# Down projection by seven products for 20 of its 43 k tiles, with earlier state loads, moved cache copies and two output tiles in two parts

## The chip, the cores and the metric

The kernel runs on one core of one Trainium2 chip. The metric is the device time of one execution in microseconds (us); less is better. The times before are 2527.97, 2526.18 and 2524.59 us, median 2526.18.

## What is computed

One inference step of one decoder layer in fp32, for a prompt of 512 tokens and 8 samples of 4 tokens (544 rows in all). Cut to what matters here:

```python
y = concat([o_a, o_b]) @ w_out            # o_a: gated linear attention, o_b: dilated attention
h = h + y                                 # D_MODEL = 2048
up = rmsnorm(h) @ w_up                    # 2048 -> 2 * 5504
full = concat([conv_hist, up])            # state: the last two rows
conv = conv_b + sum(conv_w[j] * full[:, j:j + t] for j in range(3))
u, g = split(conv)
h = h + (silu(g) * u) @ w_down            # 5504 -> 2048
y = rmsnorm(h)
k_s, v_s = old cache rows shifted by 4, with the new rows behind them   # new caches of the samples
```

Outputs are y, the attention states and caches, and the convolution's state.

## The kernel before

Activations lie transposed, 128 features on the partitions and 544 rows (NT) along the free axis, in two halves of 272 columns (HT). Each fp32 matrix product is made of three products of rounded parts: weights and activations are split into a high part (ACT, whi or ah, L190) and a low part (DVE, wlo or al, L191), and PE adds hi x hi, hi x lo and lo x hi. One k tile (128 rows of a weight) against one output tile (128 columns) so costs 3 x 2 matmuls of 128x272. PE loads weights (PEld) beside the matmuls.

The program runs through input projection and attention (to about 880 us), the output projection over 16 output tiles (gemm, L219, matmuls in L225, to about 1061), the transition to the FFN, the FFN's 43 up-projection tiles (class Pair, to about 1985) and the down projection over 16 output tiles (to about 2514), with the final norm at its end.

The output projection loads xT into h (L935), adds the product (L936), stores h to the scratch tensor hscr (L937) and starts one copy of old cache rows with every second tile (keep_rows, L631; a copy is a DMA of 3060 KB from DRAM to DRAM on POOL's queue; sixteen in all, six of them here).

The FFN works by seven products instead of eight (Pair, L977): two blocks of the weight are summed before the product, by an SP load of one block and an accumulating load of the other on POOL's queue (load, L983 to L991), or by DVE (rs + ra, rs + raw). The operand of product T3, called M below, is the block sum W(0,0) + W(1,0), loaded into raw and accumulated there. Before the first tile, the constants vcv (L1086) and the states ci (L1101) are loaded; F takes ci in (L1028), and V (L1038) is the copy of a finished product that frees its PSUM bank for the next. Each finished tile a is stored to a scratch tensor adr (L1121), 43 in all; a store and the loads that follow are ordered by semaphores.

The down projection first takes three k tiles that were kept in SBUF (KEPT, 288 matmuls, L1152 to L1156), and meanwhile loads others from adr into ar on SP's queue (fetch, L1138 to L1141) and splits them into dh and dl. Then three groups of 16, 16 and 8 k tiles follow, each over all 16 output tiles: weights come through raw (three buffers) and raw3 (two), and in the first group the stored h comes back as hr (L1201 to L1203, SP's queue).

The order of the instructions on each engine comes from a scheduler with priorities (high_priority in the code); each engine executes its own list in order, and a DMA queue belongs to the engine that issues it (SP: q1, POOL: q0).

Of the kernel before, what the change touches and what calls it, by code (L numbers as in the profile page):

```python
# [17 lines left out]
P = 128  # L18
# [24 lines left out]
GATES_FIRST = 4  # L43
POOL_SPLIT = 6
NKEPT = 3
NSLOT = 11
FW = 2 + TP + NB * (2 + TS)


# [74 lines left out]
def _build(tc, nc, es, xT, st_gla, ck, cv, conv_in, vecs, w_in, w_gu, w_out, w_up, w_dn,  # L124
           t_cs, t_bp, t_masks, t_scan, t_small,
           yT, gla_p, gla_s, kT_p, k_s, vT_p, v_s, conv_out):
    def opened(*args, **kw):
        p = tc.tile_pool(*args, **kw)
        return p, p.__enter__()
# [17 lines left out]
    def hv(t):  # L147
        return t.rearrange("p (a b) -> p a b", a=2)
# [148 lines left out]
    def gps():  # L297
        return pg.tile([P, 2, 512], F32, tag="g", name="g")
# [596 lines left out]
    def factors(some, X, pool):  # L895
# [24 lines left out]
        for i in some:  # L920
# [3 lines left out]
            else:  # L924
                parts(i, T3, 2, b[i][:, 1:3])

    X = {}
    for ot in range(KD):
        ps = gps()
        gemm(ps, [wpart(w_out, order[:8], ot * P), wpart(w_out, order[8:], ot * P)], og)  # L930
        i, j = divmod(ot, 2)
        if j == 0:
            hp = HX.tile([P, 2, NT], F32, tag="h", name="h", bufs=KD // 2 + 1 - AHEAD)
        ht = hp[:, j]
        nc.gpsimd.dma_start(ht, xT[ot * P:(ot + 1) * P, :])  # L935
        nc.vector.tensor_add(hv(ht), hv(ht), ps[:, :, :HT])  # L936
        nc.gpsimd.dma_start(hscr[ot], ht)  # L937
        if ot == 0:
            nc.scalar.activation(acc2, ht, AF.Square)
        else:  # L940
            sq = htmp("sq")
            nc.scalar.activation(sq, ht, AF.Square)
            nc.vector.tensor_add(acc2, acc2, sq)
        X[i] = hp
        if ot % 2 == 1 and kept_rows:
            keep_rows()
        nc.scalar.activation(ht, ht, AF.Copy, scale=vec[:, V_FFN + ot:V_FFN + ot + 1])
        if j == 1 and i < AHEAD:
            factors([i], X, VA)
# [132 lines left out]
    nc.scalar.activation(rstdF[:, 2:2 + TP], rstd[:, :TP], AF.Copy)  # L1082
    nc.scalar.activation(rstdF[:, 2 + TP:].rearrange("p (b s) -> p b s", s=2 + TS)[:, :, 2:],
                         rstd[:, TP:].rearrange("p (b t) -> p b t", t=TS), AF.Copy)
    vcv = FP.tile([P, NVEC - V_CW], F32, name="vcv")
    nc.gpsimd.dma_start(vcv, vecs[:, V_CW:])  # L1086

    ci_v = conv_in.rearrange("p (s f) r -> p s f r", s=2)
    co_v = conv_out.rearrange("p (s f) r -> p s f r", s=2)
    def sv(x):  # L1090
        return x[:, 2 + TP:].rearrange("p (b s) -> p b s", s=2 + TS)[:, :, :TS]

    KEPT = list(range(KF - 1 - NKEPT, KF - 1))
    kept = {}
    ci = co = None
    for f, pr in enumerate(pairs):
        if f % 4 == 0:
            n = min(4, KF - f)
            ci = FP.tile([P, 2, 4, 2 * NB], F32, tag="ci", name="ci", bufs=2)
            co = FP.tile([P, 2, 4, 2 + 2 * NB], F32, tag="co", name="co", bufs=2)  # L1100
            nc.gpsimd.dma_start(ci[:, :, :n, :], ci_v[:, :, f:f + n, :])  # L1101
# [29 lines left out]
    taken = [0]

    def slot(n=0):

        pool = DS2 if n else DS
        return pool.tile([P, NT], F32R, tag="dh", name="dh"), pool.tile([P, NT], F32R, tag="dl", name="dl")

    def fetch(k, n):  # L1138
        hi, lo = slot(n)
        x = DS.tile([P, NT], F32, tag="ar", name="ar", bufs=2)  # L1140
        nc.sync.dma_start(x, adr[k])  # L1141
        split(hi, lo, x)
        return hi, lo

    h = [None] * KD
    A1 = {}
    rest = [k for k in range(KF) if k not in KEPT]
    groups = [rest[:16], rest[16:32], rest[32:]]
    with tc.high_priority(offset=min(1500, tc.cur_priority - P0)):
        for k in groups[0][:NSLOT]:  # L1150
            A1[k] = fetch(k, 0)
    for ot in range(KD):  # L1152
        ps = gps()
        gemm(ps, [wpart(w_dn, KEPT, ot * P)], kept)
        h[ot] = rows.tile([P, NT], F32, tag="R", name="h")
        nc.scalar.activation(hv(h[ot]), ps[:, :, :HT], AF.Copy)  # L1156
    closed(g0_p, re_p, va_p)
    ds2_p, DS2 = opened(name="ds2", bufs=24 - NSLOT, side="right")
    w3_p, W3 = opened(name="w3", bufs=1, side="right")
    even = [0]  # L1160

    def wraw():
        even[0] ^= 1
        if even[0]:
            return wts.tile([P, 8, P], F32, tag="raw", name="raw", bufs=3)
        return W3.tile([P, 8, P], F32, tag="raw3", name="raw3", bufs=2)

    def ctile(name):
        return W3.tile([P, NT], F32, tag="c", name=name, bufs=2)

    def wheld(w, ks, c0, n):

        raw = wraw()
        wload(raw, w, ks, c0)
        out = []
        for j in range(2):
            hi, lo = [t[:, :4 * P].rearrange("p (k c) -> p k c", k=4) for t in slot(n[j])]
            r = raw[:, 4 * j:min(4 * j + 4, len(ks)), :]
            m = r.shape[1]
            split(hi[:, :m], lo[:, :m], r)  # L1180
            out.append([(ks[4 * j + x], hi[:, x, :], lo[:, x, :]) for x in range(m)])
        return out


    where = {}
    pool_of = [0] * NSLOT + [1] * (24 - NSLOT)
    for i, k in enumerate(rest):
        where[k] = pool_of[i % 24]
    used = len(rest)
    for gi, ks in enumerate(groups):  # L1190
        A = {}
        with tc.high_priority(offset=min(2000, tc.cur_priority - P0)):
            for k in ks:
                A[k] = A1[k] if k in A1 else fetch(k, where[k])
        if gi < len(groups) - 1:
            for ot in range(KD):
                ps = gps()
                gemm(ps, [wpart(w_dn, ks[i:i + 8], ot * P) for i in range(0, len(ks), 8)], A)
                nc.vector.tensor_add(hv(h[ot]), hv(h[ot]), ps[:, :, :HT])
                if gi == 0:  # L1200
                    x = W3.tile([P, NT], F32, tag="hr", name="hr", bufs=1)  # L1201
                    nc.sync.dma_start(x, hscr[ot])
                    nc.vector.tensor_add(h[ot], h[ot], x)  # L1203


    tc.keep_in_program_order(nc.scalar.preload_act_table_set("natural_log_exp_and_others"))
# [32 lines left out]
        finish(ot, ps, 0, 2)  # L1239
    held = []  # L1240
    for i in range(HK):
        held.append(wheld(w_dn, ks, (HK + i) * P, [pool_of[(used + 2 * i + j) % 24] for j in range(2)]))
    for s in range(2):
        for ot in range(HK, KD):
            ps = gps()
# [3 lines left out]
        for ot in range(KD):  # L1249
# [5 lines left out]
    closed(w3_p, ds2_p, ds_p, rows_p, wu_p, wts_p, psu_p, psg)  # L1255


# [64 lines left out]
```

## Time and profile before

| | |
|---|---|
| median of three runs | 2526.18 us |
| profiled execution | 2525.10 us |
| its span | 2523.3 us |
| mean granted clock of TensorE | 0.991 |
| PE busy | 2462.7 us, 19479 matmuls |
| DVE, ACT, POOL busy | 1619.3, 1078.8, 435.3 us |
| moved by DMA | 427.73 MB, mean 170 GB/s |

The span is the profiled execution from its first to its last instruction; 1.8 us of the execution's own time lie around it. A row of a table of stretches gives each engine's busy time in a window; PEclk is the granted clock as a share of 2.4 GHz, and the DMA share is the mean busy share of the core's 16 DMA engines. A wait is named by the engine that waited and by the instruction whose end released it. The landing time of a DMA runs from its issue to the arrival of its last byte.

### The profile page before, as it was taken

The page shows a single profiled execution, that of the slowest core. Times are in us where ns is not written, and L with a number is a line of the kernel's source. Part 1 is how long each engine was busy: PE and PEld are TensorE (multiplying, and loading weights), DVE is VectorE, ACT ScalarE, POOL GpSimd, SP SyncE. Part 2 cuts the span into 40 slices and gives each one's busy share as a digit, 9 for nine tenths or more (in the row PEclk, how much of TensorE's full clock was granted, in tenths as well). Part 3 has the DMA queues.
Part 4 walks back from the last instruction along what each step waited for, and adds up shares of the span by engine and source line. Part 5 has one row for each costly group of instructions (what it writes and reads, how often), then busy time and mean ns, then how long its engine had stood idle before and what let it go on. Part 6 is the DMA issues. An engine that isn't in the chain of part 4 may idle for free.

```text
span 2523.3 us, 47163 instructions
## 1 busy us (share of the span) xinstructions
PE 2462.7 (98%) x19479; PEld 2385.2 (95%) x19479; DVE 1619.3 (64%) x2460; ACT 1078.8 (43%) x1870; POOL 435.3 (17%) x581
## 2 busy tenths in 40 slices
PE   8999999999999899989999999999999999999997
PEld 8988887899999899989999999999999999999997
DVE  7777764267777843478878888888888643342243
ACT  6344464133334433355555555555555531131142
POOL 1333434210002320112212221222121000000001
PEclk9999999999999999999999999999999999999999
DMA  7777744544555498668888888889888473443232
GB/s 220 197 202 197 193 114 138 161 131 141 166 177 177 159 305 256 169 146 192 192 188 192 191 191 189 191 191 192 189 191 178 124 219 107 115 151 92 85 100 72
DMA packets 581593, 427.73 MB, mean 170 GB/s; under 512 B 18976, under 2 KB 553728, under 8 KB 580608
## 3 DMA queue, kind: packets, MB, share of 16 engines
q1 hardware_dynamic: 462144, 248.31, 34.9%
q0 software_dynamic: 115200, 171.02, 30.1%
q10 hardware_dynamic: 4032, 5.38, 0.6%
q8 instruction: 153, 2.51, 0.4%
q14 instruction: 64, 0.52, 0.1%
HBM read 397.40 MB, written 77.37 MB: 188 GB/s over the span
## 4 chain that ended last, share of the span: by engine, by line
PE 82%; DMA 8%; DVE 6%; issue 2%; POOL 1%; ACT 1%; SPq 0%; DVEq 0%; POOLq 0%; ACTq 0%
PE g L225 40%; PE b L965 20%; PE g L965 15%; DMA q<-qscr 6%; DVE pr L411 1%; PE v L507 1%; PE s L673 1%; DMA ar<-adr 1%; DVE wlo L191 1%; DVE kv L412 1%; PE s L561 1%; DMA xr<-in_xT_dram 0%; PE s L548 0%; PE s L795 0%; POOL q L408 0%
## 5 line engine op out<-in xcount | busy, mean ns | idle before, releaser
L191 DVE TENSOR_TENSOR wlo<-raw,whi 128x1024 fp32r<-128x1024 f32 (+1 forms) x341 | 408.3, 1198 | 295.6 <-ACT whi L190 288.7
L190 ACT ACTIVATE whi<-raw 128x1024 fp32r<-128x1024 f32 (+1 forms) x345 | 355.0, 1030 | 555.1 <-PE g L225 454.0
L225 PE MATMUL g<-ah,whi 128*128 128x272 f32 x2048 | 442.9, 296 | 9.8 <-ACT ah L190 4.6
L225 PE MATMUL g<-al,whi 128*128 128x272 f32 x2048 | 447.2, 297 | 0.5 <-DVE al L191 0.5
L225 PE MATMUL g<-ah,wlo 128*128 128x272 f32 x2048 | 442.4, 295 | 0.3 <-DVE wlo L191 0.3
L965 PE MATMUL b<-vh,whi 128*128 128x272 f32 x1376 | 395.1, 288 | 6.2 <-ACT V L1038 4.8
L965 PE MATMUL b<-vl,whi 128*128 128x272 f32 x1376 | 395.9, 289 | 0.8 <-DVE vl L893 0.6
L965 PE MATMUL b<-vh,wlo 128*128 128x272 f32 x1376 | 389.9, 288 | 1.3 <-DVE wlo L191 1.3
L225 PEld LDWEIGHTS g<-ah,whi 128*128 128x128 f32 x2048 | 327.9, 191 | 19.7 <-issue 10.3
L225 PEld LDWEIGHTS g<-al,whi 128*128 128x128 f32 x2048 | 329.2, 191 | 11.6 <-issue 9.3
L225 PEld LDWEIGHTS g<-ah,wlo 128*128 128x128 f32 x2048 | 328.3, 190 | 10.2 <-issue 8.5
L965 PE MATMUL g<-vl,whi 128*128 128x272 f32 x1032 | 298.8, 290 | 2.0 <-DVE vl L893 1.9
L965 PE MATMUL g<-vh,whi 128*128 128x272 f32 x1032 | 297.8, 289 | 0.4 <-ACT vh L892 0.3
L965 PE MATMUL g<-vh,wlo 128*128 128x272 f32 x1032 | 296.8, 288 | 0.0
L965 PEld LDWEIGHTS b<-vh,whi 128*128 128x128 f32 x1376 | 260.0, 189 | 6.7 <-ACT V L1038 5.1
L225 PE MATMUL g<-dh,whi 128*128 128x272 f32 x1248 | 258.0, 288 | 4.1 <-ACT whi L190 2.7
L965 PEld LDWEIGHTS b<-vl,whi 128*128 128x128 f32 x1376 | 259.5, 189 | 1.5 <-DVE vl L893 1.5
L965 PEld LDWEIGHTS b<-vh,wlo 128*128 128x128 f32 x1376 | 257.4, 189 | 1.5 <-DVE wlo L191 1.5
L225 PE MATMUL g<-dh,wlo 128*128 128x272 f32 x1248 | 258.2, 288 | 0.0
L225 PE MATMUL g<-dl,whi 128*128 128x272 f32 x1248 | 258.1, 288 | 0.0
L190 ACT ACTIVATE whi<-rs 128x1024 fp32r<-128x1024 f32 x129 | 136.8, 1061 | 266.8 <-PE g L965 201.1
L225 PEld LDWEIGHTS g<-dh,whi 128*128 128x128 f32 x1248 | 195.7, 188 | 5.4 <-ACT whi L190 3.4
(341 smaller groups left out, 4101.5 us busy)
## 6 DMA issues: line engine op xcount, KB each, us to landing
raw<-in_w_up_dram SPq DMA_DIRECT2D x129, 512.0 KB, 4.1
raw<-in_w_in_dram SPq DMA_DIRECT2D x96, 512.0 KB, 4.8
raw<-in_w_dn_dram SPq DMA_DIRECT2D x64, 512.0 KB, 4.0
out_k_s_dram<-in_ck_dram POOLq DMA_DIRECT2D x8, 3060.0 KB, 12.7
out_v_s_dram<-in_cv_dram POOLq DMA_DIRECT2D x8, 3060.0 KB, 14.5
ra<-in_w_up_dram SPq DMA_DIRECT2D x43, 512.0 KB, 7.9
rs<-in_w_up_dram SPq DMA_DIRECT2D x43, 512.0 KB, 3.8
rs<-in_w_up_dram POOLq DMA_DIRECT2D x43, 512.0 KB, 9.8
```

The source lines that it names most:

```text
L190: nc.scalar.activation(hi, src, AF.Copy)
L191: eng.tensor_sub(lo, src, hi.bitcast(F32))
L225: nc.tensor.matmul(ps[:, s, :HT], a, b[:, s * HT:(s + 1) * HT], start=(i == 0 and n == 0), stop=(i == len(todo) - 1 and n == 2))
L411: nc.vector.tensor_mul(pr, kt[:, 4:5, :].broadcast_to([P, TS, QC]), q5[:, 1:5, :])
L412: nc.vector.tensor_mul(kt[:, 0:4, :], kt[:, 0:4, :], q5[:, 0:1, :].broadcast_to([P, 4, QC]))
L507: nc.tensor.matmul(psv[32 * m:32 * m + 32, :QC], lhs, rhs, start=(kt == 0), stop=(kt == 5), tile_position=(0, 32 * m))
L561: nc.tensor.matmul(psc[r, :P], vt[:, j * P + 64 * e:j * P + 64 * e + 64], t[:, j * P:(j + 1) * P], start=(j == 0), stop=(j == qi))
L673: nc.tensor.matmul(ps[:, c * P:(c + 1) * P], KS[:, c * P:(c + 1) * P], Q[:, :, c * 64:(c + 1) * 64], start=True, stop=True)
L965: nc.tensor.matmul(b[:, :HT], a_[:, i, :], x_[i][:, v, :], start=(first and i == 0 and n == 0), stop=(i == 7 and n == 2), skip_group_check ...
```

## The change

It does four things.

1. Down projection. After the three kept k tiles the other 40 are taken as 7 plain, 10 by seven products, 7 plain, 10 by seven products, and 6 plain. A seven-product group runs over 8 pairs of output tiles (class Rows); its left operands are weight blocks of 128x5x128 (loaded, summed by an accumulating load or by DVE, split), its right operands combinations of the halves of two k tiles (right_factors), kept in ten tiles sv. Each product is 5 x 3 matmuls. Weights all go through the three buffers raw; raw3 and the pool ds2 are gone, and ar has four buffers.
2. Copies. The six copies of cache rows that went with the output projection's tiles are issued in the first plain group, before the hr loads of every second tile; hr loads go to POOL's queue and have two buffers.
3. States. vcv and the first ci are loaded when the output projection begins.
4. Two tiles. The first two tiles of the output projection are written as two parts each: all units but the last two of both tiles, then the last two of both.

```diff
+    vcv = wu.tile([P, NVEC - V_CW], F32, name="vcv")
+    nc.gpsimd.dma_start(vcv, vecs[:, V_CW:])
...
+    state = states(0)
...
+    starts = two_tiles(w_out, order, og, 2)
     for ot in range(KD):
-        ps = gps()
-        gemm(ps, [wpart(w_out, order[:8], ot * P), wpart(w_out, order[8:], ot * P)], og)
+        if ot < 2:
+            ps = starts[ot]
...
-        if ot % 2 == 1 and kept_rows:
-            keep_rows()
...
+    others = [k for k in range(KF) if k not in KEPT]
+    NP2 = 5
+    plain = (others[:NSLOT], others[NSLOT + 2 * NP2:2 * NSLOT + 2 * NP2])
+    first_of = (NSLOT, 2 * NSLOT + 2 * NP2)
+    ks = others[2 * NSLOT + 4 * NP2:]
...
+    def right_factors(k):
+
+        x, y = astage(k), astage(k + 1)
+        H, L = stile(), stile()
+        b = [x[:, :HT], x[:, HT:], y[:, :HT], y[:, HT:]]
+
+        def two(v, src):
+            nc.scalar.activation(H[:, v], src, AF.Copy)
+            nc.vector.tensor_sub(L[:, v], src, H[:, v].bitcast(F32))
+
+        two(B11, b[0])
+        nc.vector.tensor_sub(b[0], b[0], b[1])
+        two(T1, b[0])
...
+    class Rows:
...
+        def load(self, *parts, x=None):
+            x = wraw()[:, :NP2] if x is None else x
+            for n, (side, t) in enumerate(parts):
+                c0 = (2 * self.o + side) * P
+                (nc.gpsimd if n else nc.sync).dma_start(x, self.w[t][:, :, c0:c0 + P], **({"accum_op": OP.add} if n else {}))
+            return x
...
+        def p1(self):
+            with ahead():
+                self.a11 = self.load((0, 0))
+                A_ = self.cut(self.a11)
+            self.b0 = pu.tile([P, 512], F32, tag="b0", name="b0", bufs=2)
+            self.product(self.b0, A_, B11)
...
+        def others(self, then):
+            with ahead():
+                self.s = self.load((1, 0), (1, 1), x=W3.tile([P, NP2, P], F32, tag="rs", name="rs", bufs=2))
+                A_ = self.cut(self.s)
+            g = gps()
+            z, y = g[:, 0], g[:, 1]
+            self.product(z, A_, T1)
+            with ahead():
+                nc.vector.tensor_add(self.s, self.s, self.a11)
+                A_ = self.cut(self.s)
+            self.product(self.b0, A_, T2, False)
...
+            with ahead():
+                a12 = self.load((0, 1))
+                A_ = self.cut(a12)
+            self.product(y, A_, B21)
...
+            with ahead():
+                nc.vector.tensor_add(self.s, self.s, a12)
+                A_ = self.cut(self.load((0, 0), (1, 0)))
+            self.product(self.b0, A_, T3, False)
...
+            if then is not None:
+                then.p1()
+            with ahead():
+                A_ = self.cut(self.s)
+            self.product(z, A_, B22, False)
...
+            with ahead():
+                A_ = self.cut(self.load((1, 1)))
+            self.product(self.b0, A_, T4, False)
...
-    for gi, ks in enumerate(groups):
...
+    for gi in range(2):
+        for ot in range(KD):
+            ps = gps()
+            gemm(ps, [wpart(w_dn, plain[gi], ot * P)], A)
+            nc.vector.tensor_add(hv(h[ot]), hv(h[ot]), ps[:, :, :HT])
+            if gi == 0:
+                x = ctile("hr")
+                if ot % 2 == 1 and kept_rows:
+                    keep_rows()
+                nc.gpsimd.dma_start(x, hscr[ot])
+                nc.vector.tensor_add(h[ot], h[ot], x)
+            if ot == 0:
+                with late(400):
+                    fac = [right_factors(first_of[gi] + 2 * i) for i in range(NP2)]
+        rowpairs = [Rows(o_, first_of[gi], fac) for o_ in range(KD // 2)]
+        rowpairs[0].p1()
+        for i, rp in enumerate(rowpairs):
+            rp.others(rowpairs[i + 1] if i + 1 < len(rowpairs) else None)
```

Three places show how the instructions move. The first is POOL where the output projection begins; before (a row names the line, the operation, what is written and read, its shape, and how often it stands there in a row):

```order
285 L772 DMA out_gla_s_dram<-S_8289 128x8x128
286 L634 DMA out_v_s_dram<-in_cv_dram 48x16320
287 L935 DMA h<-in_xT_dram 128x544 x10
288 L991 DMA rs<-in_w_up_dram 128x8x128
289 L937 DMA hscr_9219<-h 128x544
290 L937 DMA hscr_9220<-h 128x544
291 L634 DMA out_k_s_dram<-in_ck_dram 48x16320
292 L937 DMA hscr_9221<-h 128x544
```

and now:

```order
285 L773 DMA out_gla_s_dram<-S_8289 128x8x128
286 L635 DMA out_v_s_dram<-in_cv_dram 48x16320
287 L929 DMA vcv<-in_vecs_dram 128x344
288 L938 DMA ci<-in_conv_in_dram 128x2x64 x2
289 L972 DMA h<-in_xT_dram 128x544 x10
290 L1026 DMA rs<-in_w_up_dram 128x8x128
291 L974 DMA hscr_9219<-h 128x544
292 L974 DMA hscr_9220<-h 128x544
293 L974 DMA hscr_9221<-h 128x544
```

Three loads stand ahead of the h loads, and the copy (out_k_s) between the hscr stores is gone. The second place is POOL where the down projection begins; adr_9277 is the last of the stored factors (adr42). Before:

```order
501 L991 DMA raw<-in_w_up_dram 128x8x128
502 L1027 MEMSET F 128x2 x2
503 L1124 DMA out_conv_out_dram<-co 256x1x54
504 L1121 DMA adr_9277<-a 128x544
505 L1251 TENSOR_TENSOR h<-h,rstd 128x272 x10
```

and now:

```order
494 L1026 DMA raw<-in_w_up_dram 128x8x128
495 L1062 MEMSET F 128x2 x2
496 L1323 DMA hr<-hscr_9219 128x544
497 L635 DMA out_k_s_dram<-in_ck_dram 48x16320
498 L1323 DMA hr<-hscr_9220 128x544
499 L1230 DMA rs<-in_w_dn_dram 128x5x128 x2
500 L1151 DMA out_conv_out_dram<-co 256x1x54
501 L1148 DMA adr_9277<-a 128x544
502 L1323 DMA hr<-hscr_9221 128x544
503 L635 DMA out_v_s_dram<-in_cv_dram 48x16320
```

Two hr loads, a copy and two accumulating loads now stand ahead of the store of adr42. The third place is DVE in the steady part of a seven-product group, one row pair and the first instructions of the next; there is nothing like it before:

```order
2199 L192 TENSOR_TENSOR wlo<-rs,whi 128x640
2200 L1263 TENSOR_TENSOR rs<-rs,raw 128x640
2201 L1290 TENSOR_TENSOR h<-h,g 128x272
2202 L1291 TENSOR_TENSOR h<-h,U 128x272
2203 L192 TENSOR_TENSOR wlo<-rs,whi 128x640
2204 L1296 TENSOR_TENSOR h<-h,b_24216 128x272
2205 L192 TENSOR_TENSOR wlo<-raw,whi 128x640
2206 L1276 TENSOR_TENSOR rs<-rs,raw 128x640
2207 L192 TENSOR_TENSOR wlo<-raw,whi 128x640 x2
2208 L1273 TENSOR_TENSOR h<-h,g 128x272
2209 L1282 TENSOR_TENSOR h<-h,g 128x272
2210 L1274 TENSOR_TENSOR h<-h,V 128x272
```

Row 2207 holds the low parts of M (for T3) and of the next pair's first operand; the three h updates stand between it and the split of rs for B22, after which the split of raw for the last product follows.

## Rows read from the trace of the kernel before

**Rows 1.** The page, busy time of each engine.

```profile
PE 2462.7 (98%) x19479; PEld 2385.2 (95%) x19479; DVE 1619.3 (64%) x2460; ACT 1078.8 (43%) x1870; POOL 435.3 (17%) x581
```

**Rows 2.** Table of stretches: PE, PEld, DVE, ACT, POOL busy (count), PEclk, DMA share, GB/s.

```profile
1300.00:1700.00 400.00, 400.00 (x3200) 400.00 (x3199) 320.44 (x439) 206.54 (x363) 81.23 (x105) 1.00 0.89 191
2100.00:2220.00 120.00, 120.00 (x960) 120.00 (x960) 40.55 (x45) 23.59 (x25) 0.00 (x0) 1.00 0.42 119
```

**Rows 3.** Around 1090 us: PE's wait, POOL and ACT in time, two stretches.

```profile
PE b L965 <- ACT V L1038: 4.8, 1, 4.8
...
1088.35 0.59 POOL L1086 DMA_DIRECT2D vcv<-in_vecs_dram  x1 [2.01 <-DVE rstd L171]
1088.92 0.73 POOL L1101 DMA_DIRECT2D ci<-in_conv_in_dram  x1
...
1094.00 0.32 ACT L1028 ACTIVATE F<-ci 128x16 f32<-128x16 f32 x2 [4.77 <-DMA ci<-in_conv_in_dram]
1094.23 1.04 ACT L190 ACTIVATE whi<-raw 128x1024 fp32r<-128x1024 f32 x1
...
1090.00:1096.00 6.00, 1.15 (x9) 0.94 (x7) 0.70 (x1) 2.00 (x5) 2.02 (x2) 0.83 0.56 152
1096.00:1102.00 6.00, 5.88 (x30) 5.56 (x30) 3.58 (x6) 1.21 (x4) 0.00 (x0) 0.60 1.14 212
```

**Rows 4.** Where the down projection begins: two stretches, and PE's waits in 1980 to 2045.

```profile
1980.00:2021.00 41.00, 39.63 (x312) 39.00 (x311) 20.87 (x37) 23.54 (x46) 1.32 (x2) 1.00 0.59 170
2021.00:2036.00 15.00, 12.83 (x89) 12.39 (x88) 7.26 (x9) 7.16 (x10) 0.00 (x0) 0.89 0.92 263
...
PE g L225 <- ACT whi L190: 2.2, 2, 2.0
PE g L225 <- ACT h L1156: 1.4, 2, 1.1
```

**Rows 5.** Groups by shape: splits and an update (count, busy us, mean ns, idle before).

```profile
L191 DVE TENSOR_TENSOR wlo<-raw,whi 128x1024 fp32r<-128x1024 f32 x58 | 70.9, 1222 | 25.9 <-ACT whi L190 25.9
L1030 DVE TENSOR_TENSOR F<-g,V 128x272 f32<-128x272 f32 x19 | 8.2, 434 | 0.0
...
L191 DVE TENSOR_TENSOR dl<-ar,dh 128x544 fp32r<-128x544 f32 x26 | 18.4, 723 | 22.8 <-ACT dh L190 22.8
...
L190 ACT ACTIVATE whi<-raw 128x1024 fp32r<-128x1024 f32 x57 | 59.9, 1051 | 29.9 <-issue 29.9
```

**Rows 6.** Where the output projection begins: POOL and DVE in time, PE's wait.

```profile
883.48 4.31 POOL L935 DMA_DIRECT2D h<-in_xT_dram  x8 [17.29 <-issue]
...
880.10 1.36 DVE L822 TENSOR_TENSOR oa<-oa,r 128x544 f32<-128x544 f32 x2
...
PE g L225 <- DVE h L936: 3.1, 1, 3.1
```

**Rows 7.** A stretch with one copy, and the copies' DMA issues on the page.

```profile
948.00:972.00 24.00, 24.00 (x194) 24.00 (x193) 11.54 (x17) 9.13 (x14) 2.73 (x5) 1.00 0.86 266
...
out_k_s_dram<-in_ck_dram POOLq DMA_DIRECT2D x8, 3060.0 KB, 12.7
out_v_s_dram<-in_cv_dram POOLq DMA_DIRECT2D x8, 3060.0 KB, 14.5
```

**Rows 8.** The last store of a factor (tile adr), and landings in 1985 to 2000.

```profile
L1121 POOL DMA_DIRECT2D adr<-a x1: 597/597/597, 1994.2 to 1994.2; - x1
...
raw<-in_w_dn_dram SPq DMA_DIRECT2D x7, 192.0 KB, 2.6
...
adr<-a POOLq DMA_DIRECT2D x1, 272.0 KB, 2.6
```

**Rows 9.** M in one FFN tile: SP and POOL in time; landings in 1300 to 1700.

```profile
1405.78 0.37 SPq L989 DMA_DIRECT2D raw<-in_w_up_dram  x1
...
1410.68 1.55 POOL L991 DMA_DIRECT2D raw<-in_w_up_dram  x1 [3.29 <-DMA raw<-in_w_up_dram]
...
raw<-in_w_up_dram POOLq DMA_DIRECT2D x19, 512.0 KB, 7.0
rs<-in_w_up_dram POOLq DMA_DIRECT2D x19, 512.0 KB, 9.8
```

More of the change, by code (lines that the diff above doesn't have):

```diff
@@ L45 @@
 NKEPT = 3
-NSLOT = 11
+NSLOT = 7
+NAR = 4
 FW = 2 + TP + NB * (2 + TS)
@@ L925, in factors, with states, two_tiles @@
                 parts(i, T3, 2, b[i][:, 1:3])
+    vcv = wu.tile([P, NVEC - V_CW], F32, name="vcv")
+    nc.gpsimd.dma_start(vcv, vecs[:, V_CW:])
+    ci_v = conv_in.rearrange("p (s f) r -> p s f r", s=2)
+    co_v = conv_out.rearrange("p (s f) r -> p s f r", s=2)
+    def states(f):
+        n = min(4, KF - f)
+        ci = wu.tile([P, 2, 4, 2 * NB], F32, tag="ci", name="ci", bufs=2)
+        co = wu.tile([P, 2, 4, 2 + 2 * NB], F32, tag="co", name="co", bufs=2)
+        nc.gpsimd.dma_start(ci[:, :, :n, :], ci_v[:, :, f:f + n, :])
+        return ci, co
+    state = states(0)
+    def two_tiles(w, order, X, n):
+        out = []
+        for ot in range(2):
+            units = [u for ks in (order[:8], order[8:]) for u in wpart(w, ks, ot * P)]
+            out.append((gps(), units))
+        for part in range(2):
+            for ps, units in out:
+                m = len(units) - n
+                for i, (k, hi, lo) in list(enumerate(units))[m * part:(m, None)[part]]:
+                    xh, xl = X[k]
+                    for j, (a, b) in enumerate(((hi, xh), (hi, xl), (lo, xh))):
+                        for s in range(2):
+                            nc.tensor.matmul(ps[:, s, :HT], a, b[:, s * HT:(s + 1) * HT], start=(i == 0 and j == 0),
+                                             stop=(i == len(units) - 1 and j == 2), skip_group_check=True)
+        return [ps for ps, units in out]
     X = {}
+    starts = two_tiles(w_out, order, og, 2)
     for ot in range(KD):
-        ps = gps()
-        gemm(ps, [wpart(w_out, order[:8], ot * P), wpart(w_out, order[8:], ot * P)], og)
+        if ot < 2:
+            ps = starts[ot]
+        else:
+            ps = gps()
+            gemm(ps, [wpart(w_out, order[:8], ot * P), wpart(w_out, order[8:], ot * P)], og)
         i, j = divmod(ot, 2)
@@ L1084, in _build @@
                          rstd[:, TP:].rearrange("p (b t) -> p b t", t=TS), AF.Copy)
[L1085 to L1089, printed above, removed]
     def sv(x):
@@ L1094, in _build @@
     kept = {}
-    ci = co = None
     for f, pr in enumerate(pairs):
         if f % 4 == 0:
[L1098 to L1101, printed above, removed]
+            ci, co = states(f) if f else state
         pr.ci, pr.co = ci[:, :, f % 4, :], co[:, :, f % 4, :]
@@ L1129, in _build, with late, astage, fetch @@
     ds_p, DS = opened(name="ds", bufs=NSLOT)
[L1131 to L1140, printed above, removed]
-        nc.sync.dma_start(x, adr[k])
-        split(hi, lo, x)
-        return hi, lo
[L1145 to L1151, printed above, removed]
+    h = [None] * KD
+    others = [k for k in range(KF) if k not in KEPT]
[3 more added lines that the diff above has]
+    ks = others[2 * NSLOT + 4 * NP2:]
+    assert len(ks) <= NSLOT
+    def late(n=2000):
+        return tc.high_priority(offset=min(n, tc.cur_priority - P0))
+    def astage(k):
+        x = DS.tile([P, NT], F32, tag="ar", name="ar", bufs=NAR)
+        nc.sync.dma_start(x, adr[k])
+        return x
+    def fetch(k):
+        hi = DS.tile([P, NT], F32R, tag="dh", name="dh")
+        lo = DS.tile([P, NT], F32R, tag="dl", name="dl")
+        split(hi, lo, astage(k))
+        return hi, lo
+    with late():
+        A = {k: fetch(k) for k in plain[0]}
     for ot in range(KD):
@@ L1157, in _build, with stile @@
     closed(g0_p, re_p, va_p)
-    ds2_p, DS2 = opened(name="ds2", bufs=24 - NSLOT, side="right")
     w3_p, W3 = opened(name="w3", bufs=1, side="right")
[L1160 to L1166, printed above, removed]
+    sv_p, SV = opened(name="sv", bufs=2 * NP2, side="right")
     def ctile(name):
         return W3.tile([P, NT], F32, tag="c", name=name, bufs=2)
-    def wheld(w, ks, c0, n):
+    def stile():
+        return SV.tile([P, 7, HT], F32R, tag="sv", name="sv")
@@ new lines, in right_factors @@
+    def right_factors(k):
[8 more added lines that the diff above has]
+        two(T1, b[0])
+        nc.vector.scalar_tensor_tensor(b[0], b[0], -1.0, b[3], op0=OP.mult, op1=OP.subtract)
+        two(T2, b[0])
+        two(B21, b[2])
+        nc.vector.tensor_sub(b[1], b[3], b[1])
+        two(T3, b[1])
+        two(B22, b[3])
+        nc.vector.scalar_tensor_tensor(b[2], b[0], -1.0, b[2], op0=OP.mult, op1=OP.subtract)
+        two(T4, b[2])
+        return H, L
@@ L1173, in wheld, with wsplit2 @@
+    def wsplit2(raw):
+        hi = wts.tile([P, 8, P], F32R, tag="whi", name="whi")
+        lo = wts.tile([P, 8, P], F32R, tag="wlo", name="wlo")
+        split(hi[:, :NP2], lo[:, :NP2], raw)
+        return hi, lo
+    def wheld(w, ks, c0):
+        m = len(ks)
         raw = wraw()
         wload(raw, w, ks, c0)
[L1175 to L1189, printed above, removed]
-    for gi, ks in enumerate(groups):
[L1191 to L1203, printed above, removed]
+        t = stile().rearrange("p a b -> p (a b)")
@@ new lines, in wheld @@
+        hi, lo = [t[:, x * m * P:(x + 1) * m * P].rearrange("p (k c) -> p k c", k=m) for x in range(2)]
+        split(hi, lo, raw[:, :m])
+        return [[(k, hi[:, i], lo[:, i]) for i, k in enumerate(ks)]]
+    for gi in range(2):
+        for ot in range(KD):
+            ps = gps()
+            gemm(ps, [wpart(w_dn, plain[gi], ot * P)], A)
[13 more added lines that the diff above has]
+            rp.others(rowpairs[i + 1] if i + 1 < len(rowpairs) else None)
+            if i == 0:
+                with late(400):
+                    A = {k: fetch(k) for k in (plain[1] if gi == 0 else ks)}
@@ L1241, in _build @@
     for i in range(HK):
-        held.append(wheld(w_dn, ks, (HK + i) * P, [pool_of[(used + 2 * i + j) % 24] for j in range(2)]))
+        held.append(wheld(w_dn, ks, (HK + i) * P))
     for s in range(2):
@@ L1254, in _build @@
             (nc.sync if ot % 2 else nc.scalar).dma_start(yT[ot * P:(ot + 1) * P, c], h[ot][:, c])
-    closed(w3_p, ds2_p, ds_p, rows_p, wu_p, wts_p, psu_p, psg)
+    closed(sv_p, w3_p, ds_p, rows_p, wu_p, wts_p, psu_p, psg)
 def kernel(**inputs):
```

31 lines of the change are left out of this document (added).

## The prediction

> **What bounds the kernel now.** I read the page first. PE is busy 98% of the span [rows 1], so any gain is a matmul that is not issued or a PE gap that closes. The profiled execution took 2525.1 us, 1.1 us under the median of the runs shown (2526.18); the sum starts from 2525.1. About 0.2% (5 us) can be told from no change.
>
> Next I read the table of stretches. In undisturbed stretches PE issues 8 matmuls of 128x272 per us, in the plain down projection (960 in 120 us) as in the seven-product FFN (3200 in 400 us) [rows 2]: 0.125 us each, at a granted clock of 1.00, the 2.4 GHz level. The FFN's DMA share is 0.89 there, the plain down projection's only 0.42: seven-product code needs far more DMA per PE time. PE loses time at two places that the change touches: around 1090 us [rows 3], and where the down projection begins [rows 4]. Whatever is off PE matters only where its result comes late; I followed each such result back to its last wait.
>
> **The change part by part.**
>
> *Fewer matmuls.* Twenty k tiles go from plain products to seven: per two row tiles, 20 x 2 x 6 = 240 matmuls become 2 groups x 7 products x 15 = 210; over 8 such pairs 1920 become 1680. 240 x 0.125 = **-30.0 us**. A row pair (105 matmuls) lasts 13.1 us of PE. ACT and DVE fit: seven splits of 640 columns lie between the 544 and 1024 column rows, about 0.73 us on ACT and 0.82 on DVE [rows 5]; with two adds (0.82) and seven updates of 272 columns (0.43) DVE has 7 x 0.82 + 1.64 + 3.0 = 10.4 us of work per 13.1, ACT about 6.
>
> *Early table and states.* PE waits 4.8 us for V [rows 3]: ACT stands behind F, which waits for ci, issued at 1088.92 and landed at 1094.0. In 1090 to 1102 PE issued 9 + 30 matmuls where 96 fit, a loss of 57 x 0.125 = 7.1 us; the clock in the second half was 0.60, between the levels of 1.2 and 2.4 GHz. Loaded 200 us earlier, ci is there; late next is the split of raw ahead of V (1.04 us), which leaves about 0.9 us. **-6.2 us** (bounds -3.9, the gap alone, to -7.1).
> Its price: the three DMAs stand ahead of the first h loads on POOL (first place shown above). vcv took 0.59 us of POOL and a ci 0.73 [rows 3], 2.0 us for the three; POOL had been idle for 17.29 us before the h loads [rows 6], but vcv now waits for the old tiles' last reader (DVE until 881.5 [rows 6]) and the h loads follow 2.0 us later. PE waited 3.1 us there for h [rows 6]: **+1.0 us** (0 to 2).
>
> *First output tiles in two parts.* PE's order of matmuls stands tile for tile as before until the down projection; the scheduler had interleaved those two tiles already. Zero.
>
> *Six copies moved.* Where they were, PE issued 194 matmuls in 24 us under them [rows 7], the full 192: taking them away earns nothing. Where they go there are three effects.
> First, adr42, the last stored factor (second place shown above). Before, it was issued at 1994.2 and landed in 2.6 us [rows 8]. Now the first copy stands two DMAs earlier on the same queue: issued at about 1984, landing 12.7 to 14.5 us later [rows 7], then hr1, two accumulating loads and co; adr42 lands at about 2004 rather than 1996.8. SP's first ar load waits for it, and behind that on SP stand the weights of kept tiles 10 to 15. Tile 10 is PE's at 1985 + 10 x 2.25 = 2007.5; its load (2.6 us [rows 8]) and split then end at about 2008, and the loads behind it have lost their lead. **+4 us** (0, if the small store slips through; 10, with a clock drop as in the second stretch of [rows 4], after a wait of 2.0 us).
> Second, in the first plain group a copy falls due every two tiles, 10.5 us, and takes 12.7 to 14.5: each is 2.2 to 4 us later than the one before. hr loads stand behind it on POOL's queue; DVE may fall some four tiles behind before the next weight split stands behind a late add. Third, POOL issues the first accumulating load for M only behind hr13, whose buffer waits for hr11, behind the last copy: by 11 to 20 us of lateness it lands at 2097 to 2107, needed at 2112. Together **+3 us** (0 to 15).
>
> *The wait that takes the place of the matmuls.* The third place shown above. Each row pair needs M, the sum of two weight blocks: an SP load, then an accumulating load on POOL's queue. Its buffer is the one of the operand of the previous pair's last product, so M's load starts only when DVE has split that (wlo behind wlo of B22), and that split's own buffer comes free when the previous T3 ends. So the time from one T3 to the next cannot be under: split on ACT and DVE 1.7 + load and accumulate + split of M 0.8 + T3 itself, 15 matmuls, 1.9. The FFN's load and accumulate of 512 KB took 11.9 us: issued at 1405.78, accumulate at 1410.68, landing 7.0 later [rows 9]. For 320 KB that is 7.4 us if all of it goes with bytes, 11.9 if none does; I take 9.6, the middle, since the other two accumulating rows differ by 2.8 us by what stands before them on the queue. Cycle 1.7 + 9.6 + 0.8 + 1.9 = 14.0 us, against 13.1 of PE work: 0.9 us per cycle. There are 7 cycles in each group, 14: **+12.6 us** (0 at 7.4; at 11.9 and three updates of 0.43 ahead of wlo, 17.6 us, 14 x 4.5 = 63). Waits of up to 1.1 us left the clock at 1.00 in 1980 to 2021 [rows 4], so I add nothing for the clock.
>
> The right factors (7 copies, 11 subtractions of 272 columns for each of 10 k pairs) lie in the plain stages, where DVE is busy 40.6 of 120 us [rows 2]: 5 x 11 x 0.43 = 24 us more in 84 us leaves it cover. The last group of 6 k tiles instead of 8 ends with the same tail. Zero.
>
> **Sum:** 2525.1 - 30.0 - 6.2 + 1.0 + 4.0 + 3.0 + 12.6 = 2509.5, say **2510**, 0.6% below.
>
> **Rivals.**
> *A, M comes in time.* If load and accumulate take at most 8.7 us, the cycle is 13.1 and only the smaller costs are left: 2525.1 - 36.2 + 8 = **2497**. For it: DMA demand per PE time is that of the FFN, which kept its 8 matmuls per us. Against it: there M's load did not wait for the pair's other operands. The Trainium skill, "DMA: Bandwidth & Descriptors", section "Anatomy of one DMA", fits a DMA from GpSimd as 2.0 us plus bytes over 436 GB/s; by that estimate 320 KB takes 2.75 us, the path 5.5 and the cycle 9.9, which is this rival. The rows disagree for accumulating loads: by that fit 512 KB takes 3.2 us, and they took 7.0 and 9.8 [rows 9].
> *B, slower.* M's accumulate stands behind that of the next rs on POOL and on its queue, the 2.8 us by which 9.8 exceeds 7.0. With 2.2 of it the cycle is 16.2 us: 14 x 3.1 = 43 us, time 2497 + 43 = **2540**. It decides from a cycle of 13.1 + 28.2 / 14 = 15.1 us, where the change earns nothing. For it: POOL is in order, rs comes first in every cycle. Against it: 320 KB is not 512.
> *C, the copies cost more.* If kept tiles lose 10 us, the plain group and the first M 15, with M as forecast: 2510 + 6 + 12 = **2528**, no change. For it: DMA share was 0.86 with copies at one per 24 us of PE [rows 7], now one per 10.5. Against it: nobody waits for a copy itself, and four tiles of cover stand between.
> *D, the early loads do nothing*, if V waits next for the weights of the next product, which also came then: 2516, inside the forecast's range.
>
> **How the numbers follow.** Forecast 0.50 (2500 to 2521 on its own, with D in it), A 0.18, B 0.20, C 0.12. Faster by over 0.2% means under 2521: all of A and nearly all of the forecast, 0.66. Within 0.2%: most of C and the edge of B, 0.13. Slower: B and the rest of C, 0.21. Range 2490 to 2542: below lies the case in which every cost is nil (2489), above the long end of M's cycle.
>
> **What would show it.** Right: matmuls 240 fewer; no wait for V at 1090 and its clock at 1.00; in row pairs one PE wait per 14.0 us, for whi or wlo of raw (M), and POOL's accumulates landing 9 to 10 us after M's load; adr42 landing after 2002. Wrong: row pairs of 13.1 us without waits (A), pairs over 15 us or a clock under 1.00 in them (B), the first plain group well over 84 us (C), or a new wait at the start of the output projection of several us.

## The result and the profile after

The changed kernel took 2594.77 us (median of 4 runs, 2590.25 to 2596.71) against 2525.39 before: 1.0271 times as long, 95% interval 1.0253 to 1.0289. It was forecast 0.6% faster, and the range ended at 2542 us. The profiled execution's span is 2594.9 us, 71.6 us longer than that of before.

The page of the changed kernel, busy time of each engine:

```profile
PE 2464.5 (95%) x19239; PEld 2382.8 (92%) x19239; DVE 1749.6 (67%) x2766; ACT 1143.1 (44%) x2040; POOL 490.5 (19%) x629
```

Against [rows 1] the 240 matmuls are gone, as counted, and yet PE's busy time has not fallen. Some matmuls must have run slowly, and the share of busy time fell from 98% to 95%.

The table of stretches of the changed kernel, cut at its stages (columns as in [rows 2]):

```profile
1978.00:2032.00 54.00, 43.23 (x320) 42.35 (x321) 20.87 (x38) 24.24 (x48) 6.14 (x7) 0.91 0.81 233
2032.00:2135.00 103.00, 92.15 (x687) 91.18 (x686) 55.61 (x101) 30.94 (x58) 8.69 (x16) 0.93 0.84 281
2135.00:2283.00 148.00, 122.21 (x852) 119.55 (x851) 84.53 (x139) 50.24 (x89) 25.57 (x19) 0.88 0.67 143
2283.00:2366.00 83.00, 83.00 (x666) 83.00 (x665) 49.89 (x92) 28.19 (x51) 1.48 (x1) 1.00 0.48 128
2366.00:2503.00 137.00, 115.04 (x850) 113.32 (x849) 78.68 (x130) 49.13 (x84) 19.28 (x13) 0.93 0.61 127
```

The rows are the kept tiles, the first plain group, the first eight row pairs, the second plain group and the other eight row pairs. At 8 matmuls per us the plain groups (672) need 84 us and eight row pairs (840) 105. The second plain group, with no copies in it, lasts 84 us. The first lasts 103, with the copies; the row pairs 148 and 137, 18.4 and 17.0 us each instead of 13.1. So the loss is 75 us in the row pairs, 19 in the first plain group (the kernel before itself loses some 4 us where its first group begins: 89 matmuls in 15 us where 120 fit [rows 4]) and some 12 in the kept tiles (42 to 43 us before). In the row pairs PE is busy for 122 + 115 = 237 us where 210 would do: of the 75 us some 48 are gaps and 27 are slower matmuls. In the row pairs the granted clock is 0.88 and 0.93, and the DMA share only 0.6 to 0.7: the DMA engines are not the limit there.

PE's waits from 860 us to the end (us in total, times, longest):

```profile
PE b L1240 <- ACT whi L191: 41.8, 13, 5.0
PE g L226 <- ACT whi L191: 12.9, 3, 8.0
PE g L226 <- DVE h L1318: 6.5, 3, 5.3
PE g L226 <- DVE h L973: 4.9, 1, 4.9
PE b L1240 <- ACT U L1267: 4.6, 2, 3.0
```

L1240 are the matmuls of the row pairs: PE waits 13 times for a split on ACT. Which split it is, and what it waits for, the instructions of one pair show. ACT in time:

```profile
2201.16 1.36 ACT L191 ACTIVATE whi<-raw 128x640 fp32r<-128x640 f32 x2 [8.57 <-DMA raw<-in_w_dn_dram]
2202.43 0.38 ACT L1267 ACTIVATE U<-b 128x272 f32<-128x272 f32 x1
...
2206.61 0.74 ACT L191 ACTIVATE whi<-raw 128x640 fp32r<-128x640 f32 x1 [3.18 <-PE b L1240]
...
2218.74 1.36 ACT L191 ACTIVATE whi<-raw 128x640 fp32r<-128x640 f32 x2 [5.91 <-DMA raw<-in_w_dn_dram]
```

PE in time, the first matmuls after the wait and two behind them:

```profile
2202.58 1.28 PE L1240 MATMUL b<-sv,whi 128*128 128x272 f32 x4 [4.99 <-ACT whi L191]
2203.65 0.43 PE L1240 MATMUL b<-sv,wlo 128*128 128x272 f32 x1
2203.88 0.66 PE L1240 MATMUL b<-sv,whi 128*128 128x272 f32 x2
...
2209.62 0.29 PE L1240 MATMUL g<-sv,wlo 128*128 128x272 f32 x1
```

SP's and POOL's part of the same cycle, in time:

```profile
2208.24 0.37 SPq L1230 DMA_DIRECT2D raw<-in_w_dn_dram  x1
...
2212.63 1.47 POOL L1230 DMA_DIRECT2D raw<-in_w_dn_dram  x1 [1.92 <-DVE wlo L192]
```

At 2201.16 M has landed; ACT splits it and, right behind it, the next pair's first operand. PE's list has two matmuls with that second operand ahead of T3, so PE starts at 2202.58, after 4.99 us without work. Then 17 matmuls take 3.8 us where 2.1 would be usual; one shows 0.43 us instead of the 0.29 of 2209.62. The granted clock says why:

```profile
2202.60:2206.40 3.80, 3.80 (x17) 3.80 (x18) 2.67 (x6) 0.83 (x2) 0.00 (x0) 0.50 0.32 88
2206.40:2217.80 11.40, 11.40 (x90) 11.21 (x89) 6.36 (x10) 3.53 (x6) 2.94 (x2) 0.99 0.85 154
```

0.50 is the 1.2 GHz level, after the 5 us in which PE issued nothing. When T3 ends, ACT can split the last product's operand (2206.61, released by PE), DVE follows, and its end frees the buffer: SP issues M's load at 2208.24, POOL the accumulate at 2212.63, and M has landed at 2218.74. The cycle is 1.42 (the two splits, until PE starts) + 4.03 (the two matmuls and T3) + 1.63 (split of the last product's operand) + 4.39 (from M's load to its accumulate) + 6.11 (accumulate) = 17.58 us, all in series.

In the kept tiles the landings of the DMAs issued from 1984 to 1990 speak (count, KB, median us to landing):

```profile
out_k_s_dram<-in_ck_dram POOLq DMA_DIRECT2D x1, 3060.0 KB, 15.5
rs<-in_w_dn_dram SPq DMA_DIRECT2D x2, 320.0 KB, 10.7
hr<-hscr POOLq DMA_DIRECT2D x2, 272.0 KB, 11.1
raw<-in_w_dn_dram SPq DMA_DIRECT2D x2, 192.0 KB, 17.2
rs<-in_w_dn_dram POOLq DMA_DIRECT2D x1, 320.0 KB, 16.4
```

The weights of the next kept tiles, 192 KB on SP's own queue, took 17.2 us, where they took 2.6 before [rows 8]; PE waited 8.0 us for them. The store of adr42 was issued at 2003.46 and the first ar load at 2009.18, later than the forecast's 2004 for the store's landing. But PE's wait of 8.0 us had begun at about 1996 and ended at 2003.97, so adr42 was not its cause.

### The profile page after: what moved, and what is told of

It is laid out like the page before. It is cut to its first block, busy times and chain, and to the rows that moved or that the text cites. A ratio compares the mean times of both kernels' runs of the same rounds, so it can differ in the third digit from the quotient of the medians.

```text
span 2594.9 us, 47523 instructions
## 1 busy us (share of the span) xinstructions
PE 2464.5 (95%) x19239; PEld 2382.8 (92%) x19239; DVE 1749.6 (67%) x2766; ACT 1143.1 (44%) x2040; POOL 490.5 (19%) x629
## 4 chain that ended last, share of the span: by engine, by line
PE 73%; DMA 14%; DVE 7%; issue 3%; ACT 2%; POOL 1%; SPq 0%; ACTq 0%; DVEq 0%; POOLq 0%
PE g L226 26%; PE b L1000 20%; PE g L1000 15%; DMA raw<-in_w_dn_dram 6%; DMA q<-qscr 5%; PE b L1240 4%; DVE wlo L192 2%; ACT whi L191 1%; PE g L1240 1%; PE v L508 1%; DMA ar<-adr 1%; PE s L674 1%; DVE pr L412 1%; PE s L562 1%; DMA rs<-in_w_dn_dram 1%
## 5 line engine op out<-in xcount | busy, mean ns | idle before, releaser
L192 DVE TENSOR_TENSOR wlo<-raw,whi 128x1024 fp32r<-128x1024 f32 (+4 forms) x373 | 413.9, 1113 | 289.1 <-ACT whi L191 283.8
L191 ACT ACTIVATE whi<-raw 128x1024 fp32r<-128x1024 f32 (+4 forms) x377 | 361.6, 963 | 530.1 <-PE g L226 245.9
L226 PE MATMUL g<-ah,whi 128*128 128x272 f32 x1984 | 427.6, 294 | 6.8 <-DVE h L973 4.9
L226 PE MATMUL g<-al,whi 128*128 128x272 f32 x1984 | 431.0, 295 | 0.0
L226 PE MATMUL g<-ah,wlo 128*128 128x272 f32 x1984 | 426.4, 294 | 0.0
L191 ACT ACTIVATE whi<-rs 128x1024 fp32r<-128x1024 f32 (+1 forms) x177 | 172.2, 973 | 309.4 <-PE g L1000 203.3
L192 DVE TENSOR_TENSOR wlo<-rs,whi 128x1024 fp32r<-128x1024 f32 (+1 forms) x177 | 197.2, 1114 | 39.6 <-ACT whi L191 38.1
L1000 PEld LDWEIGHTS g<-vl,whi 128*128 128x128 f32 x1032 | 195.6, 190 | 2.6 <-DVE vl L894 2.6
L1000 PEld LDWEIGHTS g<-vh,wlo 128*128 128x128 f32 x1032 | 195.8, 190 | 0.0
L1000 PEld LDWEIGHTS g<-vh,whi 128*128 128x128 f32 x1032 | 195.2, 189 | 0.7 <-ACT whi L191 0.6
## 6 DMA issues: line engine op xcount, KB each, us to landing
out_k_s_dram<-in_ck_dram POOLq DMA_DIRECT2D x8, 3060.0 KB, 12.6
```

The costliest lines, as they stand in the source:

```text
L1000: nc.tensor.matmul(b[:, :HT], a_[:, i, :], x_[i][:, v, :], start=(first and i == 0 and n == 0), stop=(i == 7 and n == 2), skip_group_check ...
```

## The experiments

Theory 1: the change has two separate losses. M's serial cycle through the shared buffer costs about 73 us in the row pairs, the copies about 30 in the kept tiles and the first plain group. Rivals, with the numbers that the expectations give them: the order on POOL's queue and not the copies (2); DMA bandwidth or DVE as the limit of the row pairs (3); ACT's order as the limit (9). The ratios are to the kernel before as measured beside each run, with medians of 2522.41 to 2523.58 us; beside the change it was 2525.39.

**Copies put back.** The copy goes back behind every second output tile of the output projection:

```diff
         X[i] = hp
+        if ot % 2 == 1 and kept_rows:
+            keep_rows()
...
                 x = ctile("hr")
-                if ot % 2 == 1 and kept_rows:
-                    keep_rows()
                 nc.gpsimd.dma_start(x, hscr[ot])
```

> The changed kernel with the six cache copies put back into the output projection; hr loads stay on POOL's queue. Theory 1 (two separate losses: the copies starve the weight and ar loads of the kept tiles and the first plain group, about 30 us; the wait for M takes about 73 us of the row pairs): kept tiles 36 to 40 us instead of 46, first plain group 84 to 88 us instead of 104, row pairs still near 17.6 us each, in all 2563 to 2572 us. Rival 2 (the queue order is at fault, hr loads and the late store of adr42 on POOL's queue, not the copies): kept tiles and first plain group keep more than half of their loss, 2580 us or more.

2559.83 us, 35 us less, 3 below the forecast. The kept tiles and the first plain group, in the table of stretches of this run, one kind of matmul in the row pairs (least, median and greatest ns, first and last start), and the landings of loads of 192 KB from 1984 to 1990:

```profile
1978.00:2020.00 42.00, 39.12 (x305) 38.16 (x304) 19.40 (x35) 22.48 (x44) 5.56 (x6) 1.00 0.81 216
2020.00:2106.00 86.00, 86.00 (x690) 86.00 (x689) 59.11 (x107) 32.05 (x58) 9.15 (x15) 1.00 0.58 167
...
L1242 PE MATMUL b<-sv,whi x640: 283/288/596, 2106.8 to 2469.0; 128*128 128x272 f32 x160
...
raw<-in_w_dn_dram SPq DMA_DIRECT2D x3, 192.0 KB, 5.0
```

Both are back to what they were or would be without waits, with hr still on POOL's queue. The loads of 192 KB land in 5.0 us, with the same hr and summed loads beside them but no copy; so of the way from 2.6 to 17.2 us most is the copy's. The row pairs, here 2106.8 to 2469.0 with the plain group between them, are as slow as before (362 us; 367 in the change). Theory 1 holds for the copies and rival 2 falls.

**M in its own buffer.**

```diff
-                A_ = self.cut(self.load((0, 0), (1, 0)))
+                A_ = self.cut(self.load((0, 0), (1, 0), x=W3.tile([P, NP2, P], F32, tag="m", name="m", bufs=1)))
```

> The changed kernel with M in a buffer of its own (one buffer of 128x5x128) instead of the three shared raw buffers. Theory 1 (the cycle from one T3 to the next through the shared buffer sets the pace): row pairs fall from 17.6 to 13.1 to 14.5 us, 2525 to 2545 us in all with the copies' loss left. Rival 3 (DMA bandwidth or DVE limits the row pairs, whatever buffer M has): row pairs stay over 16.5 us, 2580 us or more.

2527.65 us (2525.71 to 2533.87), 67 us less than the change and 1.0023 times the kernel before, interval 1.0013 to 1.0034. The table of stretches of this run, first plain group and first eight row pairs:

```profile
2032.00:2134.00 102.00, 90.40 (x682) 89.44 (x681) 55.62 (x102) 30.11 (x57) 8.76 (x16) 0.93 0.84 285
2134.00:2239.00 105.00, 103.56 (x817) 102.78 (x816) 81.09 (x133) 48.35 (x81) 22.65 (x17) 1.00 0.87 188
```

The row pairs run at PE's pace, clock 1.00, with a DMA share of 0.87 and DVE busy for 81 of 105 us: neither was the limit, and rival 3 falls. M's load may now start as soon as the previous M is split, one product T3 and one split earlier than the last operand's; with its load in time, PE has almost no gap (1.4 us in 105), and T3 is fast. The accumulating loads of m took 7.0 us there, no less than in the change.

**M without the accumulating load.** Copies back, M in the shared buffer, loaded by SP alone (this kernel leaves the second block out of M, so its down projection has other values):

```diff
-                A_ = self.cut(self.load((0, 0), (1, 0)))
+                A_ = self.cut(self.load((0, 0)))
```

> Copies back in the output projection, M in the shared buffers as in the change, but loaded by SP alone: the accumulating second block is left out (it leaves W(1,0) out of M, so the down projection's values are others). Theory 1 (the legs of the cycle are serial: split, load, accumulate, split, T3; 17.6 us in the change, of which the accumulate is 6.1 and POOL's share 0.4): the cycle would be 11.1 us, under PE's 13.1, so PE no longer waits for M; first to last matmul of the row pairs 294 to 302 us instead of 362, in all 2492 to 2502 us. Rival 9 (the splits and copies that stand in order on ACT set the cycle): pairs stay over 15 us, 2520 us or more.

2497.86 us. The same kind of matmul as above, and PE's wait in the row pairs:

```profile
L1242 PE MATMUL b<-sv,whi x640: 283/288/324, 2110.1 to 2408.0; 128*128 128x272 f32 x160
...
PE g L1242 <- ACT whi L191: 1.9, 2, 1.0
```

Row pairs and the plain group between them last from 2110.1 to 2408.0, 298 us instead of 362. With one leg of 6.5 us taken out of the same chain, the same buffers and the same order on ACT, PE waits 1.9 us in all for splits in the row pairs. So it is the length of the serial chain that decides, and rival 9 falls.

**Both edits.** Copies back and M in its own buffer.

> Both edits at once: copies back in the output projection and M in a buffer of its own. Theory 1: the two losses add, 2495 to 2512 us, faster than the kernel before. Rival 3: 2550 us or more. If the losses overlap, the gain over the changed kernel is clearly less than the sum of the two single edits.

2501.37 us, ratio to before 0.9913 (0.9898 to 0.9928), that is 93 us below the change, where the two single edits give 35 and 67, in sum 102. The losses add but for 9 us. Set against the kernel before as measured beside each, the three are 91, 33 and 65 us, and 7 are left; 5 of them lie in the row pairs, which the copies put back shorten by themselves too (367 to 362 us).

**The early states alone**, in the kernel before (vcv, ci and co in the pool wu, one slot of the factors given up for their space).

```diff
-NSLOT = 11
+NSLOT = 10
...
+    vcv = wu.tile([P, NVEC - V_CW], F32, name="vcv")
+    nc.gpsimd.dma_start(vcv, vecs[:, V_CW:])
...
+    state = states(0)
     X = {}
```

> The kernel before with the early table and states alone (one of eleven slots of the down projection's factors given up for their space). Expected from the trace of the change: the wait of 4.8 us for V goes, a wait for h at the start of the output projection grows by under 2 us, 2519 to 2523 us, that is 2 to 6 us below before. Rival: the gain is eaten by the later h loads, 2525 us, no change.

2525.14 us against 2523.2, ratio 1.0009 (0.9999 to 1.0018): no gain, although the wait for V shrank from 4.8 to 0.8 us. The wait for h grew only from 3.1 [rows 6] to 3.8:

```profile
PE g L225 <- DVE h L949: 3.8, 1, 3.8
...
PE b L978 <- ACT V L1051: 0.8, 1, 0.8
```

So the later h loads, the rival here, did not eat the gain. The trace shows what did. In 400 us of the FFN PE was busy throughout, as in [rows 2], and issued fewer matmuls:

```profile
1300.00:1700.00 400.00, 400.00 (x3183) 400.00 (x3182) 319.31 (x435) 205.78 (x361) 81.14 (x105) 1.00 0.88 191
```

3183 instead of 3200, clock 1.00, no wait: each matmul takes 0.5% longer, some 4.5 us over the FFN. All kernels with the early states so far have 3183. The table vcv and the states ci and co take 3552 bytes per partition, 32 more than a multiple of 64, and the tiles allocated after them in the same direction move by as much. Three runs test this.

**The early states and 32 unused bytes; 32 and 64 unused bytes alone.**

```diff
+    wu.tile([P, 8], F32, name="pad")
     vcv = wu.tile([P, NVEC - V_CW], F32, name="vcv")
```

> The kernel before with the early table and states, and an unused tile of 32 bytes per partition ahead of them in the same pool, so that the tiles allocated after them lie at multiples of 64 bytes again, as before (the table and states take 3552 bytes, 32 more than a multiple of 64). Theory 4 (the gain of the early states, some 3 to 4 us up to the FFN, was eaten by a slower rate in the FFN, 3183 instead of 3200 matmuls in 400 us, and that comes from where the operands lie): 3200 in 400 us again, 2517 to 2522 us. Rival 5 (the rate has nothing to do with the place): 3183 again and 2523 to 2526 us.

> The kernel before with nothing but an unused tile of 32 bytes per partition in the pool that the change puts the states into. Theory 4: 3183 instead of 3200 matmuls in 400 us of the FFN, 4 to 5 us slower than before. Rival 5: 3200 and no change.

> Control for the unused tile: the kernel before with 64 bytes per partition instead of 32. Theory 4 (what counts is that the operands lie at multiples of 64 bytes): 3200 matmuls in 400 us of the FFN and no change against before. Rival 8 (any shift costs it): 3183, and 4 to 5 us more.

The matmuls of the same 400 us (1300 to 1700) and the times:

| kernel | matmuls | us | ratio to before (interval) |
|---|---|---|---|
| before | 3200 | | |
| early states | 3183 | 2525.14 | 1.0009 (0.9999 to 1.0018) |
| early states and 32 bytes | 3201 | 2519.01 | 0.9986 (0.9977 to 0.9995) |
| before and 32 bytes | 3182 | 2527.56 | 1.0017 (1.0008 to 1.0027) |
| before and 64 bytes | 3202 | 2523.56 | 1.0002 (0.9992 to 1.0012) |

Theory 4 (of the first of these expectations: what counts is where the operands lie) holds: an unused tile of 32 bytes alone slows the kernel before, and 64 bytes do nothing. In all twelve traces the kernels whose tiles are shifted by 32 bytes have 3182 or 3183, the others 3200 to 3202. So the early states are worth 0.14%, about 3.5 us (1.3 to 5.8 by the interval), and the change lost them again by where its tiles lie. Which operand of the FFN's matmuls it is was not tried.

**Shorter rows in the copies**, with M in its own buffer: two DMAs of 1020 rows of 1536 bytes for each copy of 48 rows.

```diff
+        if len(kept_rows) < 6:
+            for c in range(2):
+                cc = slice(c * 384, (c + 1) * 384)
+                tc.keep_in_program_order(nc.gpsimd.dma_start(dst[b, 0:PAST - TS, cc], src[b, TS:PAST, cc]))
+            return
```

> M in a buffer of its own, the six copies in the first plain group as in the change, but each as two DMAs of 1020 rows of 1536 bytes instead of one of 48 rows of 65 KB. Theory 6 (the long rows of a copy hold up the short loads of weights and factors on each DMA engine): kept tiles and first plain group lose 10 us less or more, 2505 to 2517 us against 2527.65 with long rows. Rival 7 (it is the bytes): 2522 us or more.

2518.63 us (2515.77 to 2519.3), 9 us less than with long rows (2527.65), between the two forecasts. The first weights behind the copy, in 1984 to 1990, still landed late:

```profile
out_k_s_dram<-in_ck_dram POOLq DMA_DIRECT2D x2, 1530.0 KB, 16.1
raw<-in_w_dn_dram SPq DMA_DIRECT2D x2, 192.0 KB, 16.4
```

So long rows are not why these loads are held up, and PE's longest wait in the kept tiles is 6.9 us, where it was 8.8 with long rows. Inconclusive: why a copy holds up the short loads of another queue so much here stays open.

**The best version.** Both edits, the unused 32 bytes, and the summed loads of the first two row pairs held back behind kept tile 8 (a one-column write from its result into the load's buffer, so that they no longer stand ahead of adr42; `first` is true for the first two pairs of the first group):

```diff
+    wu.tile([P, 8], F32, name="pad")
...
-            x = wraw()[:, :NP2] if x is None else x
+            if x is None:
+                x = wraw()[:, :NP2]
+            elif self.first:
+                nc.scalar.activation(x[:, 0, 0:1], h[8][:, 0:1], AF.Copy)
```

> Both edits (copies back, M in a buffer of its own), the unused 32 bytes, and the summed loads of the first two row pairs held back until kept tile 8 is done, so that they no longer stand ahead of the store of adr42 on POOL's queue. Theory: the FFN regains 4.5 us, the kept tiles 4 to 6 us of the 5.7 us that they still lose; 2489 to 2495 us. Rival: the held loads come too late for the first row pair, 2500 us or more.

2487.43 us, ratio to before 0.9862 (0.9846 to 0.9879): faster than both kernels, and 1.6 us below the forecast's lower end. Its stages, kept tiles, first plain group and first row pairs:

```profile
1972.00:2010.00 38.00, 37.97 (x298) 37.58 (x299) 20.17 (x37) 21.72 (x44) 2.40 (x4) 1.00 0.66 198
2010.00:2098.00 88.00, 88.00 (x706) 88.00 (x705) 60.45 (x107) 33.99 (x63) 12.30 (x17) 1.00 0.69 186
2098.00:2204.00 106.00, 104.59 (x836) 104.38 (x836) 80.21 (x130) 49.45 (x84) 20.83 (x14) 1.00 0.86 186
```

None of these stages has more than 1.4 us of waits or a lower clock. The two new edits were not run singly. The sum of the prediction without its costs was 2525.1 - 36.2 = 2488.9; the run is 35.0 us below the kernel before measured beside it. So the terms of the gain come out in sum. That is no proof of each: the early states alone gave 3.5 us (with the later h loads in it) and not 6.2 - 1.0, and this kernel also lacks waits that the kernel before has in the kept tiles and at the start of its first plain group [rows 4].

## Why the prediction was wrong, step by step

- **Fewer matmuls, -30.0:** right; 240 fewer, and the version without the new waits comes within 2 us of the sum.
- **The wait for M, +12.6:** the step that failed. The mechanism, one serial cycle through the shared buffer, was the right one; its size was not: some 74 us (147 and 136 us from the first to the last matmul of eight pairs, against 105). Of the 85 us between forecast and measurement 61 are this term, some 20 the copies and 4 the early states. Leg by leg, forecast and measured: split of the last operand 1.7 and 1.63; load and accumulate 9.6 and 10.5; split of M 0.8 and 1.42, since the next pair's first operand is split behind it and PE's list wants both; T3 1.9 and 4.03 with two matmuls ahead of it, because PE had waited 5 us and went on at the granted clock of 0.50. "Waits of up to 1.1 us left the clock at 1.00 in 1980 to 2021 [rows 4], so I add nothing for the clock" was the largest single error in it: a wait of 0.9 us in every cycle was an average of the forecast's own making, and once it is longer the slower T3 lengthens the very cycle that caused it.
- **Rival B and the range:** B's two signs, pairs over 15 us and a clock under 1.00, came. It put the cycle at 16.2 us and its chance at 0.20; the cycles were 17 to 18.4. Its reason, a delay of 2.2 us behind the accumulate of rs, is not what the cycle above shows: load and accumulate took 10.5 us, not 11.8. The long end that the term itself names, 17.6 us, equals the cycle shown by luck: its legs are others (11.9 for load and accumulate, three updates, T3 at full clock). With it the sum is 2497 + 63 = 2560; the range, which ended at 2542, left that case outside without a reason or a chance of its own, and even it is 35 us under what was measured.
- An estimate by the fit of the Trainium skill ("DMA: Bandwidth & Descriptors", section "Anatomy of one DMA") is 2.75 us for 320 KB. The rows disagree for accumulating loads here too: 6.5 us in the change, and 7.0 with M in its own buffer, where PE hardly waited for them.
- **The copies, +4 and +3:** some 12 and, against the kernel before with its own 4 us there, 15 us: over and at the upper ends of 10 and 15, and near what rival C took (10 and 15). I had counted what stands behind a copy on POOL's own queue (adr42, hr) and left SP's weights at 2.6 us; they took 17.2. A landing time measured in a stage without copies was carried into one with them, though the trace of before had one with them, in the landings from 890 to 1060 us of the output projection:

```profile
raw<-in_w_out_dram SPq DMA_DIRECT2D x12, 512.0 KB, 11.1
```

- **Early states, -6.2 + 1.0:** the wait went (0.8 us is left), the wait for h grew by 1.8 us (4.9 against 3.1 [rows 6]); then 4.5 us went in the FFN by the 32 bytes. From the start of the output projection (881.56 before, 882.57 after) to the first kept tile (1978.51 and 1978.43) 1.1 us are left of it.
- **Two tiles in two parts, 0:** PE's order is the same row for row; no run contradicts it, none tested it by itself.

## What to carry to other kernels

A buffer that is shared by operands of one cycle links their waits: write the loop out from the freed buffer to the next use, with every in-order queue's neighbours, and compare it with the work per cycle; if they are within a few us of each other, give the operand a buffer of its own, since a gap can also cost the clock (here 27 of 75 us). When a large transfer is moved into a stage, every load of that stage has to be priced at what loads took beside such a transfer, on whatever queue they are. And a tile that is only moved to another pool shifts those that are allocated behind it: count the matmuls of a stage that the change leaves alone, before and after (here 32 bytes cost 0.5% of them, 64 bytes none).

## What the runs showed of the hardware that was not expected

- 32 unused bytes per partition ahead of the FFN's tiles slow its matmuls by 0.5% (3182 against 3200 in 400 us), with the clock at 1.00 and no wait in the profile; 64 bytes don't (3202). Which operand it is was not tried.
- Beside one copy of 3060 KB from DRAM to DRAM on POOL's queue, loads of 192 KB on SP's queue took 17.2 us. They took 5.0 with the copies elsewhere, and 2.6 in the kernel before, which has no summed loads there either. Shorter rows in the copy (16.4 us) don't help. Why is open.
